# Scores and stored transposes in a mixer's tail, and a prompt's expert stage tied behind the other stream's linear attention

## The chip, the cores and the metric

The kernel runs on one core of a Trainium2 chip. The metric is the device time of one execution in microseconds (us). A core has five engines that each work through an instruction list of their own, in order: TensorE (PE, with its weight loads as PEld), VectorE (DVE), ScalarE (ACT), GpSimd (POOL) and SyncE (SP), which issues most DMAs.

## The reference

One inference step of a two-layer backbone on two streams: a prompt of 128 tokens, and a sample of 512 tokens in four blocks of 128 that also reads the prompt's cached keys, values and states. D is 1024. Each layer is a token mixer and an expert stage, each with a residual, conditioning factors and a LayerNorm.

```python
def token_mixer(...):
    q, k, v, gq, gk, gv, gout, glr, gmerge = jnp.split(h @ w_in, IN_SPLITS, axis=-1)
    ...
        attn = gqa_attend(q_r, jnp.concatenate([k_r, ctx_k], axis=1), jnp.concatenate([v, ctx_v], axis=1))
    o_f, s_f = gla_scan(gq, gk, gv, log_a[0], s0_f)
    o_b, s_b = gla_scan(jnp.flip(gq, 1), jnp.flip(gk, 1), jnp.flip(gv, 1), jnp.flip(log_a[1], 1), s0_b)
    ...
    y = (g_attn * (attn @ w_attn_o) + g_gla * (o @ w_gla_o)) @ w_out

def peer(h, wq, sub_keys, u, v):
    ...
        q = (xt @ wq).reshape(PEER_BLOCK, PEER_HEADS, 2, PEER_HALF)
        s = jnp.einsum('thpd,pnd->thpn', q, sub_keys).astype(jnp.float32)
        s1, i1 = lax.top_k(s[:, :, 0], PEER_TOPK)
        s2, i2 = lax.top_k(s[:, :, 1], PEER_TOPK)
        cand = (s1[..., :, None] + s2[..., None, :]).reshape(PEER_BLOCK, PEER_HEADS, PEER_TOPK * PEER_TOPK)
        sc, ci = lax.top_k(cand, PEER_TOPK)
        idx = jnp.take_along_axis(i1, ci // PEER_TOPK, axis=-1) * N_KEYS + jnp.take_along_axis(i2, ci % PEER_TOPK, axis=-1)
        g = jax.nn.softmax(sc, axis=-1)
        a = jax.nn.gelu(jnp.einsum('td,thkd->thk', xt, u[idx]).astype(jnp.float32))
        return jnp.einsum('thk,thkd->td', (g * a).astype(xt.dtype), v[idx])
```

Attention has 16 heads; linear attention (`gla_scan`) runs in both directions in chunks of 64. An expert stage has blocks of 128 tokens and 8 heads with two halves of 128 keys each; a head picks 16 of 16384 experts, which makes 128 dot products and 128 weighted sums per token.

## The kernel before, in words

**Stages of the sample.** Per layer the sample passes through its mixer (`mixer`, L253: linear attention, attention by groups of heads in 64 steps, the gated projections, the output projection with LayerNorm), then through its expert stage (`s_peer`, L1156). The mixer's tail projects the expert queries head by head (L779 to L791): 512 tokens at once into PSUM, a ScalarE copy to `q`, and a store of `q` to memory (`qTd`).

**Two ways through the expert stage.** Blocks 0 and 1 (`ROWS`) go by rows: GpSimd gathers, for each of the 128 chosen experts of a token, the row of `u` (`u_rows`, L911), VectorE makes a dot product of each (L917), then the same with the rows of `v` and weighted sums (`v_rows`, L947). Blocks 2 and 3 (`DENSE`) go densely (`dense`, L984): TensorE multiplies their 256 tokens with all 16384 rows of `u` (`hp`, in chunks), and with all of `v` (`vacc`). Between them stands a matrix of weights that VectorE spreads from the top-k (`spread`, L1051: `A` and `bw`, and matmuls `Gp`). The first `Gp` needs the complete top-k of both dense blocks. The dense blocks' input is loaded as rows from `h2d` and transposed on TensorE (L990 to L997).

**The top-k.** `front` (L804) takes a block's top-k in groups of heads: scores on TensorE (`sc`), two rounds of maxima on VectorE (`top16`, L796) from PSUM, the candidate sums, and one-hot steps that pick the indices (`oh`). For block 0 it runs in the query projection's loop and reads `q` where it lies (`near`); for the others SP loads `qT` from `qTd` (L820). The prompt has its own small top-k.

**The prompt.** Its single block goes by rows (`p_peer`, L1218): 128 dots and 128 weighted sums, beside the sample's next mixer. `merge` (L1233) interleaves the program's two tracks: each piece has an estimated length and a stretch in units of the sample's pieces (0 to 0.9 first mixer, 0.9 to 2 first expert stage, 2 to 2.9 second mixer, 2.9 to 4 second expert stage). The prompt's second expert stage has 2.03 to 2.75. The order that results is the order of each engine's list; `weave` does the same inside a stage, with the stretches `RF` and `FF` and the count `U0` of dots that lie in the projection loop. The prompt's gathers of a layer are also tied behind the sample's last gather of the layer before (`last_gather`, L898 and L905).

**Split weights.** The sample's weights come in two parts, `wh` (ScalarE copies) and `wl`, the rest that VectorE or GpSimd subtracts (L141).

## Time and profile before

| | |
|---|---|
| median of 3 runs | 5448.35 us (5431.43 to 5451.07) |
| profiled execution, its own time | 5425.23 us |
| span of the profile | 5423.5 us |
| TensorE busy | 4479.1 us (83%), mean granted clock 0.887 |
| VectorE busy | 3891.9 us (72%) |
| ScalarE, GpSimd busy | 1038.4 us (19%), 2199.4 us (41%) |
| moved by DMA | 1440.70 MB, 266 GB/s |

A busy share is a mean over stages with different limits. The stages of the second layer are: 2987 to 3036 us the end of layer 0, 3036 to 3516 linear attention, 3516 to 3771 attention, 3771 to 3980 gated projections, 3980 to 4063 output and LayerNorm, 4063 to 4177 query projection, top-k until the first `Gp` at 4490, dense blocks and row blocks to 5424. The prompt's second expert stage lies from 3017 to 3555. In layer 0 the attention's first 48 steps lie at 771 to 1070 and the gated projections at 1070 to 1345, there beside the prompt's first expert stage.

### The profile page before, as it was taken

What the parts mean: (1) busy time and instruction counts of PE and PEld (TensorE: products, weight loads), DVE (VectorE), ACT (ScalarE), POOL (GpSimd) and SP (SyncE); (2) the same over time, 40 slices, a digit from 0 to 9 for tenths busy, and PEclk for the clock granted to TensorE, in tenths of its full rate; (3) what the DMA queues carried; (4) which work ended last, traced back from release to release, by engine and by line L of the source; (5) the groups of instructions that cost most, each with busy time, mean ns of one, the idle gap of its engine ahead of it and who ended that gap; (6) DMA issues with size and microseconds to landing.
All of it is one profiled execution on the core that took longest, in us unless ns stands there. A gap on an engine that the chain in (4) does not pass through costs nothing.

```text
span 5423.5 us, 71661 instructions
## 1 busy us (share of the span) xinstructions
PE 4479.1 (83%) x26668; PEld 3365.0 (62%) x26668; DVE 3891.9 (72%) x8020; ACT 1038.4 (19%) x1876; POOL 2199.4 (41%) x1632
## 2 busy tenths in 40 slices
PE   7979878877766789799999477688977458998998
PEld 5658766755655657567674355588765347675643
DVE  4242578887699987948565999963258999979682
ACT  4231223412212101110000312255221010000000
POOL 0000026675255541544431576610115657255440
PEclk8989977888878889899999778789988779998999
DMA  5325669898489887899995788820447989699985
GB/s 185 118 70 179 235 225 327 305 338 297 171 318 348 317 317 258 310 357 334 382 344 206 244 309 297 290 91 29 131 146 271 329 305 362 225 399 325 409 327 197
DMA packets 472734, 1440.70 MB, mean 266 GB/s; under 512 B 55232, under 2 KB 123968, under 8 KB 472384
## 3 DMA queue, kind: packets, MB, share of 16 engines
q0 software_dynamic: 221184, 805.40, 40.5%
q1 hardware_dynamic: 251200, 630.71, 33.0%
q8 instruction: 209, 3.42, 0.2%
q14 instruction: 141, 1.16, 0.1%
HBM read 1391.29 MB, written 44.63 MB: 265 GB/s over the span
## 4 chain that ended last, share of the span: by engine, by line
PE 39%; DVE 26%; DMA 15%; issue 14%; POOL 4%; ACT 2%; SPq 0%; DVEq 0%; POOLq 0%; ACTq 0%
PE vacc L1096 7%; DVE gat L917 7%; PE gt L156 6%; PE proj L156 6%; DMA gat<-in_pv,idx 5%; PE hp L156 4%; DMA gat<-in_pu,idx 4%; POOL gat L900 4%; DVE acc L947 4%; PE po L156 3%; PE qp L156 2%; DMA v<-in_pv 2%; PE s L156 1%; PE gqk L156 1%; DVE A L1055 1%
## 5 line engine op out<-in xcount | busy, mean ns | idle before, releaser
L900 POOL DMA_INDIRECT gat<-in_pu,idx x768 | 982.3, 1279 | 884.9 <-DVE gat L917 378.7
L900 POOL DMA_INDIRECT gat<-in_pv,idx x768 | 989.4, 1288 | 765.1 <-DVE acc L947 472.9
L947 DVE SCALAR_TENSOR_TENSOR acc<-gat,dots,acc 128x1024 f32<-128x1024 f32 x762 | 1006.3, 1321 | 168.3 <-DMA gat<-in_pv,idx 156.1
L917 DVE SCALAR_TENSOR_TENSOR gat<-gat,h 128x1024 f32<-128x1024 f32 x768 | 948.4, 1247 | 110.8 <-DMA gat<-in_pu,idx 109.5
L156 PE MATMUL hp<-h2Td,uc 128*128 128x256 f32 x4096 | 942.5, 391 | 79.8 <-DVE wk L800 49.6
L1096 PE MATMUL vacc<-v,Q 128*128 128x512 f32 x2048 | 923.3, 604 | 17.2 <-DMA v<-in_pv 17.2
L156 PEld LDWEIGHTS hp<-h2Td,uc 128*128 128x128 f32 x4096 | 795.3, 196 | 200.2 <-DVE wk L800 52.3
L141 POOL TENSOR_TENSOR wl<-w,wh 128x1024 fp32r<-128x1024 f32 x92 | 227.5, 2473 | 1450.0 <-ACT wh L139 1279.5
L1096 PEld LDWEIGHTS vacc<-v,Q 128*128 128x128 f32 x2048 | 384.1, 193 | 459.4 <-issue 435.4
L139 ACT ACTIVATE wh<-w 128x1024 fp32r<-128x1024 f32 x184 | 194.4, 1058 | 631.9 <-PE proj L156 299.1
L1009 ACT ACTIVATE Q<-hp 128x512 f32<-128x512 f32 x128 | 76.4, 597 | 1069.6 <-PE hp L156 1069.3
L156 PE MATMUL proj<-wh,hTh 128*128 128x256 f32 x896 | 265.6, 296 | 5.6 <-DVE sgo L497 2.9
L156 PE MATMUL proj<-wl,hTh 128*128 128x256 f32 x896 | 264.7, 295 | 5.5 <-POOL wl L141 5.4
L156 PE MATMUL proj<-wh,hTl 128*128 128x256 f32 x896 | 262.8, 293 | 0.0
L1070 PEld LDWEIGHTS <-A 128*128 128x128 bf16 x6144 | 172.8, 97 | 125.7 <-DVE bw L1063 63.2
L156 PE MATMUL po<-V,pT 128*128 128x64 f32 x1600 | 237.9, 294 | 9.9 <-ACT pT L639 9.8
L156 PEld LDWEIGHTS po<-V,pT 128*128 128x128 f32 x1600 | 229.2, 217 | 24.9 <-ACT pT L639 16.7
L1070 PE MATMUL Gp<-bw,A 128*128 128x32 bf16 x6144 | 175.8, 177 | 73.3 <-DVE bw L1063 64.1
L141 DVE TENSOR_TENSOR wl<-w,wh 128x1024 fp32r<-128x1024 f32 x92 | 121.0, 1315 | 158.7 <-ACT wh L139 148.4
L629 DVE TENSOR_REDUCE nm<-s 128x1 f32<-128x768 f32 (+1 forms) x160 | 131.0, 820 | 139.9 <-PE s L156 138.5
L156 PEld LDWEIGHTS proj<-wh,hTh 128*128 128x128 f32 x896 | 176.9, 197 | 20.4 <-issue 16.2
L156 PEld LDWEIGHTS proj<-wl,hTh 128*128 128x128 f32 x896 | 176.9, 197 | 20.4 <-issue 13.8
(297 smaller groups left out, 7355.5 us busy)
## 6 DMA issues: line engine op xcount, KB each, us to landing
uc<-in_put SPq DMA_DIRECT2D x256, 512.0 KB, 7.0
v<-in_pv SPq DMA_DIRECT2D x256, 512.0 KB, 6.7
w<-in_win SPq DMA_DIRECT2D x208, 512.0 KB, 5.1
w<-in_adaw SPq DMA_DIRECT2D x96, 512.0 KB, 5.7
w<-in_wq SPq DMA_DIRECT2D x64, 512.0 KB, 5.8
w<-in_wgo SPq DMA_DIRECT2D x32, 512.0 KB, 5.5
w<-in_wao SPq DMA_DIRECT2D x32, 512.0 KB, 5.2
w<-in_wout SPq DMA_DIRECT2D x32, 512.0 KB, 5.5
```

The source lines that it names most:

```text
L139: nc.scalar.activation(wh, r, AF.Copy)
L141: (nc.vector, nc.gpsimd)[i].tensor_sub(wl, r, f32(wh))
L156: nc.tensor.matmul(out, lt, rt, start=(i == 0), stop=(i == n - 1))
L629: nc.vector.tensor_reduce(nm, s[:, 0:KEYS], axis=AX.X, op=OP.max, negate=True)
L900: i = nc.gpsimd.indirect_dma_start(out=t, out_offset=None, in_=src, in_offset=bass.IndirectOffsetOnAxis(ap=self.res[b][0][:, k:k + 1], axi ...
L917: nc.vector.scalar_tensor_tensor(u, u, 1.0, h2, op0=OP.mult, op1=OP.mult, accum_out=dots[:, k:k + 1])
L947: nc.vector.scalar_tensor_tensor(acc, v, w_, acc, op0=OP.mult, op1=OP.add)
L1009: nc.scalar.activation(q[:, i:i + 2, :].rearrange("p i t -> p (i t)"), t, AF.Gelu_apprx_tanh)
L1055: nc.vector.tensor_tensor(a.rearrange("p t (i w) -> p t i w", w=2), pairs[:, None].to_broadcast([128, TG, NK // 2, 2]), i1[:, sl, None, :] ...
L1070: nc.tensor.matmul(t[:, j * CI:(j + 1) * CI], a[:, j, :], bw[:, j, q, :], start=(q == 0), stop=(q == 2))
L1096: nc.tensor.matmul(accs[i][:, s * 512:(s + 1) * 512], w[:, j, i * 128:(i + 1) * 128], v[:, s * 512:(s + 1) * 512], start=(key == 0), stop= ...
```

## The change

**1. Scores in the mixer's tail.** After a head's two query projections the loop also computes the scores of all four blocks, and ScalarE copies them to `sc` in SBUF. Block 0's stay there; those of blocks 1 to 3 are stored, by ScalarE's DMA queue, to `scd`. `q` of the sample is no longer stored. `front` of these blocks loads 128 KB of scores (`scs`), also on ScalarE's queue, and `top16` reads them from SBUF, so that no matmul stands in it.

```diff
-                    nc.sync.dma_start(qTd[2 * h + k], q)
+                if tr:
+                    yield 11
+                    for b0 in range(0, nb, 2):
+                        s = psm("sc", 1)
+                        for i in range(2):
+                            for k in range(2):
+                                nc.tensor.matmul(s[:, (2 * i + k) * NK:(2 * i + k + 1) * NK],
+                                                 qs[k][:, (b0 + i) * 128:(b0 + i + 1) * 128],
+                                                 lp[l]["sk"][:, k, :], start=True, stop=True)
+                        sc = hp.tile([128, 2, 2 * NK], F32, tag="sc", bufs=4, name="sc")
+                        nc.scalar.activation(sc.rearrange("p b n -> p (b n)"), s, AF.Copy)
+                        for i in range(2):
+                            if b0 + i == ROWS[0]:
+                                lp[l]["s", h] = sc[:, i, :]
+                            else:
+                                nc.scalar.dma_start(scd[b0 + i, :, h * 2 * NK:(h + 1) * 2 * NK], sc[:, i, :])
...
+                elif tr:
+                    s = own.tile([128, 2 * NK], F32, tag="scs", bufs=2, name="scs")
+                    nc.scalar.dma_start(s, tops[tr, l][b, :, hh * 2 * NK:(hh + 1) * 2 * NK])
```

**2. Order of the dense blocks' top-k.** Their fronts work in groups of two heads and are woven into the projection loop (three of four groups each), the rest follows at once; `U0` falls, so fewer dots lie in the loop.

```diff
+NEXT = (2, 2, 2, 2)
-FF = (0.05, 0.1, 0.3, 0.46)
+FF = (0.01, 0.02, 0.3, 0.46)
-U0 = 56
+U0 = 24
+            fd = [p.front(d, NEXT) for d in DENSE]
-                for n in LEAD:
-                    yield from take(m, n)
+                for i, n in enumerate(LEAD):
+                    yield from take(m, 2 * n)
                     yield from take(f0, 3 * n + 1)
+                    if i >= 2:
+                        for f in fd:
+                            yield from take(f, 3 * NEXT[i - 2] + 1)
```

**3. The dense blocks' input stored transposed.** ScalarE copies the transposes that LayerNorm's end makes anyway (`hc`) and SP stores them to `h2t_dram`; `dense` loads them in one DMA.

```diff
+                        if kept:
+                            hc = spare("hc")
+                            nc.scalar.activation(hc[:, 0:jg * 128], t, AF.Copy)
+                            i = DENSE.index(b)
+                            nc.sync.dma_start(h2t_dram[l][:, j0:j0 + jg, i * 128:(i + 1) * 128],
+                                              hc[:, 0:jg * 128].rearrange("p (j t) -> p j t", j=jg))
...
-            for i, b in enumerate(blocks):
-                x = dp.tile([128, D], F32, tag="uv", bufs=UB, name="x")
-                nc.sync.dma_start(x, h2_dram[self.tr, self.l][b * 128:(b + 1) * 128, :])
-                t = psb("h2td")
-                for j in range(ND):
-                    nc.tensor.transpose(t[:, j * 128:(j + 1) * 128], x[:, j * 128:(j + 1) * 128], ident)
-                evac(h2T[:, :, i * 128:(i + 1) * 128], t.rearrange("p (j t) -> p j t", j=ND))
-                yield 4
+            nc.sync.dma_start(h2T, h2t_dram[self.l])
```

**4. The prompt's second expert stage.** Its stretch moves, and its gathers are tied behind the latest GpSimd instruction of the sample, a gather or a subtraction `wl`, in place of the latest gather.

```diff
-           (wait(("s_done", 0)), 1000.0, 1.95, 2.0), (p_peer(1), 386.0, 2.03, 2.75)])
+           (wait(("s_done", 0)), 1000.0, 1.95, 2.0), (p_peer(1), 386.0, 2.36, 2.86)])
-            after = last_gather.get(self.l - 1) if self.tr == 0 else None
+            after = last_pool.get("ins") if self.tr == 0 and self.l else None
```

GpSimd, from the last gather of the sample's first layer on (gathers of `in_pu` rows are for the dots, of `in_pv` rows for the sums). Before:

```order
L900 DMA gat<-in_pv,idx 128x1024 x128
L141 TENSOR_TENSOR wl<-w,wh 128x1024
L900 DMA gat<-in_pu,idx 128x1024 x17
L141 TENSOR_TENSOR wl<-w,wh 128x1024
L900 DMA gat<-in_pu,idx 128x1024 x11
L141 TENSOR_TENSOR wl<-w,wh 128x1024
L900 DMA gat<-in_pu,idx 128x1024 x5
```

And after:

```order
L937 DMA gat<-in_pv,idx 128x1024 x128
L143 TENSOR_TENSOR wl<-w,wh 128x1024 x15
L937 DMA gat<-in_pu,idx 128x1024 x9
L143 TENSOR_TENSOR wl<-w,wh 128x1024
L937 DMA gat<-in_pu,idx 128x1024 x52
L143 TENSOR_TENSOR wl<-w,wh 128x1024
L937 DMA gat<-in_pu,idx 128x1024 x47
L143 TENSOR_TENSOR wl<-w,wh 128x1024
```

The first gather for the prompt stood behind one weight part and now stands behind fifteen, those of the linear attention.

VectorE in the scan of the second linear attention (`S` is the recurrent state, L917 the prompt's dots). Before:

```order
L482 SCALAR_TENSOR_TENSOR S<-S,ee,kv 128x256 x2
L917 SCALAR_TENSOR_TENSOR gat,dots<-gat,h_22584 128x1024 x2
L482 SCALAR_TENSOR_TENSOR S<-S,ee,kv 128x256
L141 TENSOR_TENSOR wl<-w,wh 128x1024
L917 SCALAR_TENSOR_TENSOR gat,dots<-gat,h_22584 128x1024
L482 SCALAR_TENSOR_TENSOR S<-S,ee,kv 128x256 x2
L917 SCALAR_TENSOR_TENSOR gat,dots<-gat,h_22584 128x1024 x2
L482 SCALAR_TENSOR_TENSOR S<-S,ee,kv 128x256
```

And after:

```order
L426 TENSOR_TENSOR a<-eb,gq 128x512
L143 TENSOR_TENSOR wl<-w,wh 128x1024
L424 TENSOR_TENSOR m<-m,gk 128x512
L449 COPY_PREDICATED amat_22622<-masks,A 128x512
L449 COPY_PREDICATED amat_22624<-masks,A 128x512
L487 SCALAR_TENSOR_TENSOR S<-S,ee,kv 128x256 x12
L143 TENSOR_TENSOR wl<-w,wh 128x1024
L487 SCALAR_TENSOR_TENSOR S<-S,ee,kv 128x256 x2
```

No dot stands between the updates of the state any more.

TensorE from the last query projection to the first matmuls of the dense blocks (`hp`), layer 1. Before:

```order
L156 MATMUL qp<-h2Th,wl 128x512
L825 MATMUL sc<-sk,q 128x128 x2
L825 MATMUL sc<-sk,qT 128x128 x2
L995 MATMUL h2td<-ident,x 128x128 x16
L825 MATMUL sc<-sk,qT 128x128 x6
L156 MATMUL hp<-h2Td,uc 128x256 x43
L825 MATMUL sc<-sk,qT 128x128 x2
L156 MATMUL hp<-h2Td,uc 128x256 x5
```

And after:

```order
L160 MATMUL qp<-h2Tl,wh 128x512
L160 MATMUL qp<-h2Th,wl 128x512
L814 MATMUL sc<-sk,q 128x128 x8
L160 MATMUL hp<-h2Td,uc 128x256 x256
L1069 MATMUL kT<-ident,kf 128x128 x2
L1070 MATMUL kT<-ident,g 128x128
```

The transposes and the score matmuls of the dense blocks are gone from the front of `hp`; `kT` transposes the finished top-k of a dense block.

## Rows read from the trace of the kernel before

**Rows 1.** the chain of waits, share of the span by engine

```profile
PE 39%; DVE 26%; DMA 15%; issue 14%; POOL 4%; ACT 2%; SPq 0%; DVEq 0%; POOLq 0%; ACTq 0%
```

**Rows 2.** windows: length, busy time of each engine, TensorE's granted clock, DMA share, GB/s

```profile
2987.00:3036.00 49.00, 8.99 (x38) 7.32 (x38) 47.28 (x167) 16.55 (x27) 12.30 (x9) 0.57 0.56 194
3036.00:3516.00 480.00, 345.66 (x1758) 260.35 (x1758) 438.88 (x657) 114.96 (x175) 341.97 (x249) 0.80 0.86 299
3516.00:3771.00 255.00, 225.30 (x1708) 213.57 (x1708) 139.95 (x253) 138.62 (x292) 27.53 (x18) 0.89 0.20 63
3771.00:3980.00 209.00, 192.70 (x867) 156.71 (x866) 53.66 (x67) 60.65 (x82) 38.27 (x16) 0.97 0.38 121
4080.00:4490.00 410.00, 231.07 (x970) 188.01 (x969) 396.65 (x1194) 47.42 (x68) 252.46 (x192) 0.77 0.87 311
4490.00:4880.00 390.00, 381.30 (x2853) 288.83 (x2850) 345.39 (x656) 25.41 (x38) 194.71 (x144) 0.98 0.88 329
```

**Rows 3.** groups on VectorE, linear attention: busy us, mean ns, idle before, releasers

```profile
L917 DVE SCALAR_TENSOR_TENSOR gat<-gat,h 128x1024 f32<-128x1024 f32 x124 | 162.0, 1324 | 15.2 <-DMA gat<-in_pu,idx 14.8
L947 DVE SCALAR_TENSOR_TENSOR acc<-gat,dots,acc 128x1024 f32<-128x1024 f32 x107 | 145.9, 1363 | 7.3 <-DMA gat<-in_pv,idx 5.1 <-ACT acc L945 1.2
L917 DVE DVE_READ_ACCUMULATOR gat<-gat,h 128x1 f32 x124 | 9.7, 78 | 0.0
```

**Rows 4.** waits of TensorE in the linear attention: us, times, longest

```profile
PE ksT L426 <- DVE m L419: 52.6, 8, 20.8
PE oTp L505 <- DVE sgo L500: 19.2, 2, 10.2
```

**Rows 5.** groups on VectorE, attention of layer 1

```profile
L947 DVE SCALAR_TENSOR_TENSOR acc<-gat,dots,acc 128x1024 f32<-128x1024 f32 x20 | 25.5, 1277 | 0.2
```

**Rows 6.** groups on VectorE, top-k stretch of layer 1, 4080 to 4490

```profile
L917 DVE SCALAR_TENSOR_TENSOR gat<-gat,h 128x1024 f32<-128x1024 f32 x128 | 158.5, 1243 | 8.0 <-DMA gat<-in_pu,idx 7.9
L947 DVE SCALAR_TENSOR_TENSOR acc<-gat,dots,acc 128x1024 f32<-128x1024 f32 x50 | 63.6, 1273 | 0.8 <-DMA gat<-in_pv,idx 0.6
L843 DVE TENSOR_TENSOR cand<-tv 128x16 f32<-128x16 f32 (+11 forms) x63 | 11.2, 219 | 0.0
```

**Rows 7.** groups on VectorE, first 48 steps of layer 0's attention, 771 to 1070

```profile
L917 DVE SCALAR_TENSOR_TENSOR gat<-gat,h 128x1024 f32<-128x1024 f32 x127 | 154.7, 1235 | 4.5 <-DMA gat<-in_pu,idx 4.4
L947 DVE SCALAR_TENSOR_TENSOR acc<-gat,dots,acc 128x1024 f32<-128x1024 f32 x10 | 12.8, 1278 | 2.1 <-ACT acc L945 1.9
```

**Rows 8.** windows of layer 0's attention and gated stage

```profile
771.00:1070.00 299.00, 254.42 (x1713) 203.96 (x1713) 259.71 (x472) 115.06 (x242) 187.86 (x139) 0.79 0.89 320
1070.00:1345.00 275.00, 206.64 (x811) 161.20 (x809) 224.22 (x201) 60.07 (x77) 183.75 (x129) 0.84 0.88 318
```

**Rows 9.** groups on VectorE, gated stage of layer 0

```profile
L947 DVE SCALAR_TENSOR_TENSOR acc<-gat,dots,acc 128x1024 f32<-128x1024 f32 x117 | 171.2, 1463 | 27.1 <-DMA gat<-in_pv,idx 24.9
```

**Rows 10.** groups on TensorE, gated stage of layer 0

```profile
L156 PE MATMUL gt<-gxh,wh 128*128 128x512 f32 x128 | 55.6, 454 | 42.3 <-ACT gxh L271 42.3
```

**Rows 11.** groups on TensorE, gated stage of layer 1, 3771 to 3980

```profile
L156 PE MATMUL gt<-gxh,wh 128*128 128x512 f32 x128 | 50.1, 408 | 12.2 <-ACT gxh L271 12.2
```

**Rows 12.** groups on TensorE, top-k stretch of layer 1, 4080 to 4490

```profile
L156 PE MATMUL hp<-h2Td,uc 128*128 128x256 f32 x512 | 126.3, 411 | 41.2 <-DVE wk L800 24.3 <-issue 15.3 <-ACT Q L1009 1.6
L825 PE MATMUL sc<-sk,qT 128*128 128x128 f32 x64 | 16.0, 393 | 85.6 <-DVE wk L800 43.8 <-DMA qT<-qTd 39.7 <-ACT Q L1009 2.1
L825 PE MATMUL sc<-sk,q 128*128 128x128 f32 x31 | 6.4, 286 | 2.5 <-ACT q L785 2.4
L1070 PE MATMUL Gp<-bw,A 128*128 128x32 bf16 x17 | 0.6, 188 | 12.6 <-DVE bw L1063 12.6
```

**Rows 13.** groups on ScalarE, whole span

```profile
L785 ACT ACTIVATE q<-qp 128x512 f32<-128x512 f32 x32 | 18.7, 590 | 70.4 <-PE qp L156 70.4
```

**Rows 14.** DMA issues, whole span: KB each, median us to landing

```profile
qT<-qTd SPq DMA_DIRECT2D x64, 128.0 KB, 4.2
```

**Rows 15.** groups of the page, whole span

```profile
L1070 PE MATMUL Gp<-bw,A 128*128 128x32 bf16 x6144 | 175.8, 177 | 73.3 <-DVE bw L1063 64.1
```

More of the change, by code (lines that the diff above doesn't have):

```diff
@@ L119 @@
     lp = {}
+    last_pool = {}
     class Weights:
@@ L140, in __call__ @@
                 wl = self.pool.tile([128, 4, CW], F32R, tag="wl", bufs=3, name="wl")
-                (nc.vector, nc.gpsimd)[i].tensor_sub(wl, r, f32(wh))
+                ins = (nc.vector, nc.gpsimd)[i].tensor_sub(wl, r, f32(wh))
+                if i:
+                    last_pool["ins"] = ins.ins
                 h.append(wh)
@@ L314, in mixer @@
         x1_dram[tr, l], h2_dram[tr, l] = x1d, h2d
+        if tr:
+            h2t_dram[l] = dram.tile([128, ND, len(DENSE) * 128], F32, name=f"h2t{l}")
         ys_ = ExitStack()
@@ L696, in mixer @@
             yield from ada(l, (GATE1, SCALE2, SHIFT2, GATE2), W)
-        qTd = dram.tile([2 * PH, 128, T], F32, name=f"qTd{tr}{l}")
-        tops[tr, l] = qTd
+        if tr:
+            scd = dram.tile([nb, 128, PH * 2 * NK], F32, name=f"scd{l}")
+            tops[tr, l] = scd
+        else:
+            qTd = dram.tile([2 * PH, 128, T], F32, name=f"qTd{tr}{l}")
+            tops[tr, l] = qTd
         with mkp("out") as op:
@@ L757, in mixer @@
                     nc.vector.tensor_add(h2, h2, sh)
-                    nc.sync.dma_start(h2d[b * 128:(b + 1) * 128, :], h2)
+                    kept = tr == 1 and b in DENSE
+                    if not kept:
+                        nc.sync.dma_start(h2d[b * 128:(b + 1) * 128, :], h2)
                     for j0 in range(0, ND, jg):
@@ L780, in mixer @@
                 t = ptile("qp")
+                qs = []
                 for k in range(2):
                     projT(t[:, k * off:k * off + T], w, k, h2T)
-                    q = hp.tile([128, T], F32, tag="q", bufs=2 + 2 * tr, name="q")
+                    q = hp.tile([128, T], F32, tag="q", bufs=2 + tr, name="q")
                     if tr:
@@ L816, in front @@
                 if near:
-                    qs = [lp[l]["q", tr, 2 * hh + k][:, b * 128:(b + 1) * 128] for k in range(2)]
+                    s = lp[l]["s", hh]
+                elif tr:
+                    s = own.tile([128, 2 * NK], F32, tag="scs", bufs=2, name="scs")
+                    nc.scalar.dma_start(s, tops[tr, l][b, :, hh * 2 * NK:(hh + 1) * 2 * NK])
                 else:
@@ L821, in front @@
                                       .rearrange("k p t -> p k t"))
-                    qs = [qT[:, k, :] for k in range(2)]
-                s = psm("sc", tr)
-                for k in range(2):
-                    nc.tensor.matmul(s[:, k * NK:(k + 1) * NK], qs[k], lp[l]["sk"][:, k, :], start=True, stop=True)
+                    s = psm("sc", tr)
+                    for k in range(2):
+                        nc.tensor.matmul(s[:, k * NK:(k + 1) * NK], qT[:, k, :], lp[l]["sk"][:, k, :],
+                                         start=True, stop=True)
                 for k in range(2):
@@ L903, in gather @@
             if self.tr == 1:
[L904 removed]
+                last_pool["ins"] = i.ins
             return t
@@ L1162, in s_peer @@
             r0, r1 = ROWS
-            d0, d1 = DENSE
             f0, u0 = p.front(r0, LEAD, True), p.u_rows(r0)
+            fd = [p.front(d, NEXT) for d in DENSE]
             def lead():
-                for n in LEAD:
-                    yield from take(m, n)
+                for i, n in enumerate(LEAD):
+                    yield from take(m, 2 * n)
                     yield from take(f0, 3 * n + 1)
+                    if i >= 2:
+                        for f in fd:
+                            yield from take(f, 3 * NEXT[i - 2] + 1)
                 for _ in m:
                     pass
-            yield from weave([(lead(), 160.0, 0.0, 1.0)], [(take(u0, U0), 1.5 * U0, UP, 1.0)])
+            yield from weave([(lead(), 260.0, 0.0, 1.0)], [(take(u0, U0), 1.5 * U0, UP, 1.0)])
             for _ in f0:
@@ L1183, in s_peer @@
                               (p.u_rows(r1), 192.0, r[2], r[3]), (p.v_rows(r1), 197.0, r[3], r[4])],
-                             [(p.front(d0), 50.0, 0.0, f[0]), (p.front(d1), 50.0, f[0], f[1]),
-                              (p.front(r1), 50.0, f[2], f[3])])
+                             [(fd[0], 12.5, 0.0, f[0]), (fd[1], 12.5, f[0], f[1]), (p.front(r1), 50.0, f[2], f[3])])
         fs = parts["fin"] = ExitStack()
```

12 lines of the change are left out of this document (7 added, 5 removed).

## The prediction

> **What bounds the kernel now.** I read the chain of waits by engine first [rows 1]: TensorE 39%, VectorE 26%, DMA 15%, so no single engine is the bound throughout, and a change must be priced stage by stage. I then cut the part that the change touches, the sample's second layer, into stretches [rows 2]. The reader is to see who is full in each. 2987 to 3036 (residual and LayerNorm of layer 0): VectorE 47.28 of 49 us. 3036 to 3516 (linear attention): VectorE 438.88 of 480, TensorE only 345.66 at a granted clock of 0.80. 3516 to 3771 (attention): TensorE 225.30 of 255, VectorE 139.95. 3771 to 3980 (the gated projections): TensorE 192.70 of 209 at 0.97, VectorE 53.66. 4080 to 4490 (query projection and top-k ahead of the dense blocks): VectorE 396.65 of 410. From 4490 the dense blocks: TensorE 381.30 of 390. So VectorE bounds the linear attention and the top-k, TensorE the rest.
>
> What fills VectorE in the linear attention is not the sample's own work. The groups of that stretch [rows 3] show 124 dot products of the prompt's expert stage (162.0 us, and 9.7 us of accumulator reads) and 107 weighted sums (145.9 us). TensorE meanwhile waits [rows 4]: 52.6 us on `m` and 19.2 us on `sgo`, both VectorE tiles that queue behind prompt work.
>
> **The change part by part.** Baseline is the profiled execution, 5425.23 us (span 5423.5); the median of the runs is 23.1 us higher, so I add 23 at the end.
>
> *The prompt's second expert stage goes behind the second linear attention.* By the instruction order, of the 128 dots 16 come between the scan and attention, 112 in attention's first 48 head steps of 64; 26 sums lie in those steps, none in the last 16, 97 in the gated stage, the last 5 ahead of LayerNorm.
>
> Settle: 4 of the 128 dots ran before 3036, on a full VectorE. At about 1.3 us each that is -5 us (bounds -10 and 0).
>
> Linear attention: VectorE keeps 438.88 - 162.0 - 9.7 - 145.9 = 121 us, plus 16 dots (21 us), far under the stage's length, so TensorE is late next. Its 345.66 us at 0.80 become 345.66 x 0.80 / 0.97 = 285 us at the clock that the gated stage had when no prompt work stood beside it. Of its 134 us of idle I keep a third, 45 us, for the recurrence and for ScalarE. 480 becomes 330: -150 us. Lower bound: no idle left, 285 us, -195. Upper: clock unchanged and only the two VectorE waits gone, 480 - 52.6 - 19.2 = 408 us, -72.
>
> Attention: VectorE's own work is 139.95 less 20 sums (25.5 us [rows 5]) = 114.5 us. Added are 112 dots at 1.238 us and 0.078 us of accumulator read [rows 6, 3], 147.4 us, and 26 sums at 1.273 us, 33.1 us; the prices of dot and sum are from the top-k stretch [rows 6], where VectorE was full. In the first 48 steps that is 0.75 x 114.5 + 180.5 = 266 us; at the 97% that VectorE reaches when it bounds (396.65 of 410) 275 us. The last 16 are TensorE's: 225.30 x 0.89 / 0.97 / 4 = 52 us. Sum 327, +72 us. Layer 0 bounds it from above: there attention ran beside 127 dots and 10 sums [rows 7] and its first 48 steps took 299 us, TensorE at 0.79 [rows 8]: 299 + 52 = 351, +96. From below, if VectorE had no gap: 114.5 + 180.5 = 295, +40.
>
> Gated stage: layer 0 again has the case, 1070 to 1345 [rows 8]: 275 us against 209, with 117 sums at 1463 ns [rows 9], TensorE's wait for `gxh` 42.3 us in place of 12.2 [rows 10, 11], clock 0.84 in place of 0.97. That is 66 us for 117 sums; for 97, +55 us. Bounds: 66 above; below 0, because 53.66 + 97 x 1.273 = 177 us would still fit into 209.
>
> In the gated stage a sum takes 1463 ns, beside GpSimd's subtractions `wl`, and 1273 ns in the top-k stretch [rows 6, 9]. The Trainium skill, "SBUF — State Buffer", section "Who interferes with whom", says that a VectorE instruction with two SBUF inputs and a GpSimd instruction that reads SBUF exclude one another on a shared port, and that TensorE and ScalarE wait for nobody there. The longer sums of the gated stage agree. By that rule alone the stage would lose only the lock time and the sum would be that of rival B; by layer 0's whole stage it loses 55 us.
>
> *Scores in the tail.* Per layer the projection loop gains 48 score matmuls for three blocks (64 for four, 16 for one before) at 6.4 / 31 = 0.21 us [rows 12], 10 us of TensorE, and 16 ScalarE copies of about 0.59 us, as `q` has [rows 13], 9 us. Both lie beside a full VectorE, so most is hidden; 24 stores and 24 loads of 128 KB also pass through ScalarE's instruction stream. The loads wait for a buffer that VectorE must free, and behind a waiting load stand the copies that release TensorE. A load of that size took 4.2 us to land [rows 14]. I take +5 us per layer, +10 (bounds -5 and +25). The 32 stores of `q` leave SP, off any full engine: nothing.
>
> *Top-k of the dense blocks.* The 85.6 us that TensorE idled ahead of `sc<-sk,qT` and the 41.2 ahead of `hp` [rows 12] vanish as such: the 256 `hp` now follow without a break. But they open nothing: the first `Gp` needs all the top-k, and VectorE was full in that stretch. So I count VectorE's work ahead of it in both orders. Layer 0: 10 sums fewer (-13 us), about 120 more small top-k operations at 0.22 us [rows 6] (+26 us) since groups of two heads replace groups of four, 32 more maxima at the same price (+7): +20. Layer 1: 30 sums fewer (-38), the small operations +26, seven one-hot steps at no more than a dot's 1.3 us (+9): -3. Later TensorE waited 64.1 us for `bw` over both layers [rows 15], of which 12.6 was the first `Gp` of layer 1 [rows 12]; taking as much for layer 0, about 40 remain, met where block 1's top-k stood in front of the second spread. That top-k is now earlier; I take half, -20. Together -3 us (bounds -40: all 40 and nothing added; +35: VectorE's 20 in layer 0, and 15 more in layer 1, if its sums merely move).
>
> *Stored transposed input.* 16 transposes (3.4 us at the 0.21 us of a small matmul) and two evacuations leave the dense blocks' start, two ScalarE copies come in per layer, the store goes out where the row store did, and one load takes the place of two. TensorE idles over 100 us there [rows 12], so 0; without that cover the 3.4 us per layer would be gained.
>
> Sum: -5 - 150 + 72 + 55 + 10 - 3 = -21 us. 5425 - 21 = 5404 for a profiled execution, 5427 against the median.
>
> **Rivals.**
>
> *A, the attention and gated stages become VectorE's.* VectorE executes in order, so the row maximum that releases the next score tile, and the subtraction behind `gxh`, stand behind 1.3 us operations. For: layer 0 shows just this pairing, with TensorE at 0.79 and 0.84. Against: layer 0 also loaded the conditioning weights there (320 GB/s in its row against 63), which layer 1 doesn't. Attention +96, gated +66, and the linear attention loses only the wait for `m`: 285 + 134 - 53 = 366, -114. Sum -5 - 114 + 96 + 66 + 10 - 3 = +50: 5498. It decides once the linear attention takes over 340 us beside stages as in layer 0.
>
> *B, the sums fit into the gated stage's gaps.* Then it grows only by what the sums take longer there than elsewhere, 97 x (1463 - 1273) ns = 18 us, the rest as forecast: -21 - 37 = -58: 5390. The rule of the Trainium skill named above would have it so. For: VectorE is idle 155 of 209 us, and the sums' own gathers don't compete with other loads. Against: layer 0's 42.3 us on `gxh`.
>
> *C, ScalarE's queue blocks.* The 24 loads per layer hold the copies behind them. If each of the waits for `qT` (within the 85.6 us) comes back as a wait of VectorE on its scores, some 40 us per layer: +80 on the forecast, 5507. For: two buffers and one in-order queue. Against: most loads stand behind the last projection copies.
>
> *D, the tie moves the work without effect*, gain and price equal: 5448. TensorE would keep its low clock in the linear attention.
>
> **How the numbers follow.** The shortest difference that the measurement separates from no change is about 0.5%, 27 us: faster means under 5421, slower over 5476. Forecast 0.48, its own band 5395 to 5460, of it 0.22 under 5421; A 0.17; B 0.20; C 0.10 (0.07 at over 49 us, which ends slower, 0.03 below that); D 0.05. Faster: 0.22 + 0.20 = 0.42. Same: 0.26 + 0.05 + 0.03 = 0.34. Slower: 0.17 + 0.07 = 0.24. The terms' bounds as half widths (5, 61, 28, 33, 15, 37) add in squares to 85; I take 5360 to 5500, which leaves out C's full price, and the case where linear attention meets its lower bound in B.
>
> **What the profile would show.** The linear attention near 330 us with no prompt dot in its scan and a granted clock over 0.9; attention near 327 and the gated stage near 264 us; first `Gp` of layer 1 as far behind the first projection as before; no `sc<-sk,qT`. The forecast is wrong if the linear attention stays over 380 us, if the gated stage doesn't grow, or if VectorE waits on `scs`.

## The result and the profile after

The changed kernel is slower: 5479.48 us, median of 5 runs (5476.02 to 5484.05), against 5448.35 us; ratio 1.0064, 95% interval 1.0048 to 1.0079. The forecast was 5427 us, within 5360 to 5500: the sign was wrong, by a margin that the range allowed for. The profiled execution took 5484.05 us, 58.8 more than that of before. Of these some 25 belong to the profiled execution of before, which lay 6 us below the fastest of its other runs: profiled again (e1 below) the unchanged kernel had a span of 5439.5 us, and the changed one (e5) 5473.5.

Windows of the changed kernel, over the stages of [rows 2]: settle, linear attention, attention, gated stage, output and LayerNorm, top-k until the first `Gp`, dense blocks. Columns as there.

```profile
3017.00:3060.00 43.00, 10.49 (x48) 8.09 (x46) 42.97 (x173) 16.77 (x27) 2.59 (x1) 0.56 0.43 144
3060.00:3421.00 361.00, 310.01 (x1759) 238.48 (x1760) 178.76 (x337) 113.13 (x177) 61.57 (x37) 0.92 0.26 86
3421.00:3746.00 325.00, 241.03 (x1704) 221.25 (x1704) 264.03 (x462) 136.30 (x288) 168.69 (x136) 0.83 0.67 234
3746.00:4017.00 271.00, 207.12 (x843) 163.60 (x842) 182.63 (x160) 59.89 (x81) 165.02 (x116) 0.85 0.78 285
4017.00:4113.00 96.00, 56.45 (x416) 53.63 (x415) 69.45 (x99) 21.40 (x21) 10.44 (x5) 0.78 0.51 180
4130.00:4549.00 419.00, 218.43 (x971) 182.67 (x970) 398.82 (x1448) 59.54 (x90) 207.80 (x162) 0.77 0.76 270
4549.00:4940.00 391.00, 380.31 (x2864) 286.04 (x2865) 328.31 (x457) 22.57 (x35) 215.16 (x155) 0.98 0.92 340
```

The work moved as the order said. The linear attention lost 120 us (480 to 361), VectorE is no longer full there (178.76 us), and TensorE's clock rose from 0.80 to 0.92, not to 0.97. The attention took 325 us in place of 255, the gated stage 271 in place of 209. Within the attention the first 48 steps and the last 16 were:

```profile
3419.00:3706.00 287.00, 201.26 (x1368) 182.97 (x1368) 247.25 (x438) 108.78 (x228) 169.91 (x138) 0.80 0.76 264
3706.00:3748.00 42.00, 42.00 (x358) 40.51 (x356) 19.74 (x29) 30.64 (x67) 0.00 (x0) 1.00 0.04 11
```

The waits of TensorE in the linear attention show what is late next:

```profile
PE ksT L431 <- DVE m L424: 14.7, 6, 4.4
PE kTp L565 <- ACT kd L560: 12.4, 2, 12.1
```

The wait for `m` fell from 52.6 us [rows 4] to 14.7. The prompt's dots and sums on VectorE, first in the attention, then in the gated stage; before, the attention had 20 sums [rows 5] and the gated stage none:

```profile
L954 DVE SCALAR_TENSOR_TENSOR gat<-gat,h 128x1024 f32<-128x1024 f32 x111 | 133.9, 1219 | 10.7 <-DMA gat<-in_pu,idx 9.8 <-issue 0.3
L984 DVE SCALAR_TENSOR_TENSOR acc<-gat,dots,acc 128x1024 f32<-128x1024 f32 x26 | 33.4, 1283 | 2.6 <-DMA gat<-in_pv,idx 2.3
```

```profile
L984 DVE SCALAR_TENSOR_TENSOR acc<-gat,dots,acc 128x1024 f32<-128x1024 f32 x97 | 134.7, 1389 | 34.5 <-DMA gat<-in_pv,idx 32.7
```

In the gated stage TensorE waits for `gxh` as in layer 0 [rows 10, 11], and behind it ScalarE waits for the loads of `xraw`: first the group on TensorE, then two waits of ScalarE.

```profile
L160 PE MATMUL gt<-gxh,wh 128*128 128x512 f32 x128 | 53.6, 438 | 38.0 <-ACT gxh L274 38.0
```

```profile
ACT gxh L274 <- DMA xraw<-aod: 36.9, 8, 13.4
ACT gxh L274 <- DMA xraw<-ood: 32.2, 7, 12.6
```

In the kernel before, the same two waits came to 15.5 and 15.6 us.

TensorE and VectorE in the top-k stretch, against [rows 12, 6], and the page's row on `Gp` against [rows 15]:

```profile
L160 PE MATMUL hp<-h2Td,uc 128*128 128x256 f32 x512 | 123.6, 407 | 149.7 <-ACT Q L1040 83.8 <-DMA uc<-in_put 65.9
```

```profile
L984 DVE SCALAR_TENSOR_TENSOR acc<-gat,dots,acc 128x1024 f32<-128x1024 f32 x20 | 25.5, 1276 | 0.1
L835 DVE MAX8 tv<-wk 128x8 f32<-128x128 f32 x64 | 17.9, 284 | 0.0
L880 DVE TENSOR_TENSOR cand<-tv 128x16 f32<-128x16 f32 (+10 forms) x103 | 14.6, 184 | 0.0
```

```profile
L1101 PE MATMUL Gp<-bw,A 128*128 128x32 bf16 x6144 | 178.0, 177 | 76.1 <-DVE bw L1094 64.5
```

The wait for `qT` is gone, but `hp` now waits for `Q`, a ScalarE tile: that is TensorE's old slack under another name, since VectorE was busy 398.82 of 419 us. It had 20 sums there in place of 50, but 64 rounds of maxima in place of 48 and 103 candidate sums in place of 63. The wait for `bw` did not fall (64.1 to 64.5 us).

By stage, in us; "second pair" are the profiles of e1 and e5:

| stage | forecast | first pair | second pair |
|---|---|---|---|
| layer 0 until its query projection | 0 | +15.2 | -0.8 |
| layer 0, query projection to end of settle | +10 | +8.6 | +0.5 |
| linear attention | -150 | -120.4 | -121.8 |
| attention, gated stage, output, LayerNorm | +127 | +146.7 | +144.4 |
| layer 1, query projection to end | -8 | +8.7 | +11.7 |
| sum | -21 | +58.8 | +34.0 |

The second pair's sum is near the +31 of the medians, so I go by it; the 15 us ahead of layer 0's query projection were chance. Its two profiles come from two chips, but e1's profiled execution (5441.32 us) lies at the median of the kernel before on e5's chip (5442.11 us).

### The profile page after: what moved, and what is told of

Its sections match the earlier page's. It is cut to its first block, busy times and chain, and to the rows that moved or that the text cites. A ratio compares the mean times of both kernels' runs of the same rounds, so it can differ in the third digit from the quotient of the medians.

```text
span 5482.3 us, 71820 instructions
## 1 busy us (share of the span) xinstructions
PE 4440.9 (81%) x26636; PEld 3342.6 (61%) x26636; DVE 3905.8 (71%) x8202; ACT 1064.6 (19%) x1923; POOL 2150.0 (39%) x1632
## 4 chain that ended last, share of the span: by engine, by line
PE 32%; DVE 29%; issue 16%; DMA 14%; POOL 6%; ACT 3%; SPq 0%; another core or an unknown queue 0%; POOLq 0%; DVEq 0%; ACTq 0%
DVE gat L954 8%; DMA gat<-in_pv,idx 7%; PE vacc L1127 6%; PE proj L160 6%; PE gt L160 5%; POOL gat L937 5%; PE hp L160 3%; DMA gat<-in_pu,idx 3%; DVE acc L984 3%; PE po L160 2%; PE gqk L160 2%; DVE A L1086 2%; DVE Q L1106 1%; PE s L160 1%; DVE bw L1094 1%
## 5 line engine op out<-in xcount | busy, mean ns | idle before, releaser
L937 POOL DMA_INDIRECT gat<-in_pv,idx x768 | 956.3, 1245 | 892.9 <-DVE acc L984 588.7
L937 POOL DMA_INDIRECT gat<-in_pu,idx x768 | 963.6, 1255 | 823.0 <-DVE gat L954 416.2
L1101 PE MATMUL Gp<-bw,A 128*128 128x32 bf16 x6144 | 178.0, 177 | 76.1 <-DVE bw L1094 64.5
L487 DVE SCALAR_TENSOR_TENSOR S<-S,ee,kv 128x256 f32<-128x256 f32 x128 | 61.4, 479 | 177.9 <-PE kv L475 177.7
```

The costliest lines, as they stand in the source:

```text
L487: nc.vector.scalar_tensor_tensor(S2, S[d], ee_[d][:, cc:cc + 1], kv[d][:, 0:DV], op0=OP.mult, op1=OP.add)
L937: i = nc.gpsimd.indirect_dma_start(out=t, out_offset=None, in_=src, in_offset=bass.IndirectOffsetOnAxis(ap=self.res[b][0][:, k:k + 1], axi ...
L1101: nc.tensor.matmul(t[:, j * CI:(j + 1) * CI], a[:, j, :], bw[:, j, q, :], start=(q == 0), stop=(q == 2))
```

## The experiments

T1 is the reading of the stage table: the tie's loss of 147 us behind the linear attention outweighs its gain. R2 is its rival: the tie gains, and the scores and their order lose. Ratios are against runs of the kernel before on the same chip, in brackets their 95% intervals.

**e1, the kernel before once more.**

> The unchanged kernel once more, for a second profile. Theory T1 (the changed kernel's first layer is really slower ahead of its dense blocks) expects the stage map of the first profile: first query projection of layer 0 at about 1428 us, of layer 1 at 4063. Rival R1 (some 25 of the 59 us between the two profiles belong to the profiled run of before, which lay 23 us under its median) expects a span near 5446 and these points 10 to 25 us later. Ratio 1.000 within 0.003 by both.

Measured: 0.9996 (0.9981 to 1.0011), span 5439.5 us, first query projections at 1435.0 and 4076.8. Nearer to R1, at less than it expected: these points came 6.6 and 13.5 us later than in the first profile, and nothing under some 15 us per stage can be read from a single pair.

**e2, the tie alone** (part 4 on the kernel before).

```diff
-            after = last_gather.get(self.l - 1) if self.tr == 0 else None
+            after = last_pool.get("ins") if self.tr == 0 and self.l else None
...
-           (wait(("s_done", 0)), 1000.0, 1.95, 2.0), (p_peer(1), 386.0, 2.03, 2.75)])
+           (wait(("s_done", 0)), 1000.0, 1.95, 2.0), (p_peer(1), 386.0, 2.36, 2.86)])
```

> The kernel before with part 4 alone (prompt's second expert stage at 2.36 to 2.86 and tied behind the latest GpSimd instruction). Theory T1, from the stages of the changed kernel's profile: linear attention -120 us, attention and gated stage +136, output and LayerNorm +11, settle -7, so +20 us, ratio 1.004, and the linear attention at about 360 us. Rival R2 (the tie gains, scores and order lose): -20 us, 0.996. Forecast on record: -28 us.

Measured: 1.0039 (1.0025 to 1.0053), +21 us. T1 held, R2 fell: the part of the change on which the forecast's gain rested loses by itself. Its windows, linear attention, attention and gated stage, are those of the changed kernel:

```profile
3040.00:3400.00 360.00, 310.59 (x1762) 238.57 (x1762) 176.03 (x334) 113.09 (x177) 62.27 (x38) 0.92 0.26 86
3400.00:3729.00 329.00, 241.84 (x1714) 222.69 (x1712) 264.60 (x463) 137.57 (x291) 174.37 (x136) 0.82 0.67 231
3729.00:3995.00 266.00, 203.01 (x839) 159.60 (x839) 185.96 (x161) 58.98 (x80) 165.99 (x117) 0.87 0.80 291
```

**e3, the changed kernel without the tie** (e2's edit undone).

> The changed kernel without part 4. T1: what remains of the changed kernel's +31 us once the tie's +20 is out: about +11 us, ratio 1.002, linear attention near 480 us again. R2: +50 us, 1.009. A third possibility, that parts 1 to 3 gain and the tie loses it all: below 0.998.

Measured: 1.0067 (1.0053 to 1.0081), more than T1's 1.002 and less than R2's 1.009. So parts 1 to 3 lose too, and the losses of e2 and e3 don't add up to that of the whole (1.0064 here, 1.0064 in e5). T1 was half the story; the next runs take the other half apart.

**e4, the stored transposed input alone** (part 3 on the kernel before).

> The kernel before with part 3 alone (transposed input stored in the mixer's tail, no transposes in the dense blocks). Forecast on record: 0 us. Rival R3 (the two copies by ScalarE lie on the path from LayerNorm to the query projection, which starts 15 and 19 us later in the changed kernel): up to +10 us per layer, ratio 1.002 to 1.004, with the first query projection later by that much from the gated stage's end.

Measured: 1.0000 (0.9986 to 1.0013). As forecast, nothing in the total, where R3 fell. But the place that R3 named does show: from the first output projection to the first query projection it took 89.8 us in layer 0 and 91.3 in layer 1, against 85.7 and 87.3 in e1. What gives these 4 us per layer back, or whether they vanish in the interval, was not tested.

**e5, the changed kernel once more.**

> The changed kernel once more, beside the next three on one chip. All theories: ratio 1.006 within 0.002, linear attention about 360 us, attention to query projection about 690 us, the first A of the dense blocks 404 to 421 us behind the first query projection.

Measured: 1.0064 (1.0045 to 1.0083); linear attention 361.1 us, from there to the query projection 690.5, first A 421.4 and 405.6 us behind it.

**e6, stored scores and input without the new order of the fronts.** T4: part 2 is what makes parts 1 to 3 slow; R4: the stored scores are. The edit, on e3:

```diff
-FF = (0.01, 0.02, 0.3, 0.46)
+FF = (0.05, 0.1, 0.3, 0.46)
...
-U0 = 24
+U0 = 56
...
-                    if i >= 2:
-                        for f in fd:
-                            yield from take(f, 3 * NEXT[i - 2] + 1)
...
-                             [(fd[0], 12.5, 0.0, f[0]), (fd[1], 12.5, f[0], f[1]), (p.front(r1), 50.0, f[2], f[3])])
+                             [(p.front(d0), 50.0, 0.0, f[0]), (p.front(d1), 50.0, f[0], f[1]), (p.front(r1), 50.0, f[2], f[3])])
```

> The changed kernel without parts 2 and 4: scores and transposed input from the tail, the dense blocks' top-k in groups of four heads and not in the projection loop, the prompt as before. By its instruction order VectorE has ahead of the first A 103 dots and no sum where the kernel before has 144 and 16 (layer 0) or 159 and 31 (layer 1). Theory T4 (part 2 is what makes parts 1 to 3 slow, by the extra groups and the block 1 heads that it puts ahead of the first A) expects no loss against before, ratio 0.990 to 1.000, and the first A 50 to 90 us earlier behind the first query projection. Rival R4 (the stored scores themselves, by ScalarE's queue, cost it) expects 1.004 to 1.010 and VectorE waiting on scs.

Measured: 0.9992 (0.9979 to 1.0005). T4's main point held, and R4 fell: without part 2, storing scores and input costs nothing that can be measured. But the first A, 64 us earlier in layer 0 and 99 in layer 1, brought nothing: the first `Gp` came 453 and 426 us behind the query projection (e1: 425 and 428). In the 128 and 134 us between A and `Gp` stand 25 dots, 23 to 29 sums and one-hot steps for another 8 to 10 heads. What counts is what stands ahead of the first `Gp`, not of the first A.

**e7, the new order of the fronts alone** (part 2 on the kernel before, with `qT` loads).

> The kernel before with part 2 alone: fronts of the dense blocks in groups of two heads in the projection loop, U0 24, with qT loads and score matmuls as before. Its order has 182 dots, 54 sums and 13 groups ahead of the first A (before: 144 to 159, 16 to 31, 9). T4: the first A 50 to 100 us later per layer, part of it given back in the dense blocks, ratio 1.005 to 1.015. R4: ratio 1.000 within 0.003.

Measured: 1.0231 (1.0211 to 1.0251), worse than T4 expected: first `Gp` 524 and 475 us behind the query projection, 99 and 47 later than in e1. R4 fell. Parts 1 and 2 interact: with scores at hand the new order costs 0.7%, with `qT` loads 2.3%.

**e8, the tie with short operations.** A test of rival A of the prediction: is it VectorE's occupation that lengthens the attention and the gated stage? The edit, on e2, with the like of it for the weighted sums:

```diff
+                c = 64 if self.tr == 0 and self.l == 1 else D
-                nc.vector.scalar_tensor_tensor(u, u, 1.0, h2, op0=OP.mult, op1=OP.mult, accum_out=dots[:, k:k + 1])
+                nc.vector.scalar_tensor_tensor(u[:, 0:c], u[:, 0:c], 1.0, h2[:, 0:c], op0=OP.mult, op1=OP.mult,
+                                               accum_out=dots[:, k:k + 1])
```

> The kernel before with part 4 alone, and the prompt's dots and weighted sums of layer 1 over 64 of 1024 columns (it leaves out the rest of these sums; all gathers stay). If VectorE's occupation is what makes the attention and gated stages longer (forecast, rival A of the prediction), their growth of about 136 us goes nearly all, they take 255 and 209 us again, and the ratio is 0.975 to 0.980. Rival R5 (gathers, memory traffic and the lower TensorE clock make it): they stay over 300 and 250 us, ratio over 0.995.

Measured: 0.990 (0.9875 to 0.9926). Neither: attention and gated stage fell only to 302 and 256 us, though VectorE was idle over half of both. (The profiled execution was the slowest of the four, 13 us over their median.)

```profile
3398.00:3700.00 302.00, 244.47 (x1708) 225.75 (x1709) 131.96 (x477) 137.33 (x291) 140.83 (x142) 0.85 0.74 260
3700.00:3956.00 256.00, 203.69 (x856) 162.30 (x854) 84.86 (x162) 61.07 (x82) 138.02 (x117) 0.87 0.82 306
```

In the gated stage the waits for `xraw` were 59 us (69 in e2, 31 in e1): the gathers keep them long. In the attention VectorE, with these short operations, stood 23 us waiting for gathered rows:

```profile
L920 DVE SCALAR_TENSOR_TENSOR gat<-gat,h 128x64 f32<-128x64 f32 x118 | 23.3, 218 | 26.2 <-DMA gat<-in_pu,idx 18.8 <-issue 7.5
L952 DVE SCALAR_TENSOR_TENSOR acc<-gat,dots,acc 128x64 f32<-128x64 f32 x26 | 7.2, 278 | 4.4 <-DMA gat<-in_pv,idx 4.1
```

**e9, the tie with few gathers.** On e2, with the like of it for the rows of v:

```diff
+                if k % 8 == 0 or self.tr == 1 or self.l == 0:
-                u = self.gather(pu, b, k)
+                    u = self.gather(pu, b, k)
```

> The kernel before with part 4 alone, and the prompt's stage of layer 1 gathers only every eighth row of u and v (it computes the other dots and sums from the row at hand, so the other rows are left out); all 256 VectorE operations stay. In the run with short operations the growth of attention and gated stage went down by only 42 of 139 us. Theory T5 (the gathers do the rest: their traffic delays the loads of xraw that gxh waits for in the gated stage, and VectorE waits in order for late rows) expects xraw waits back near 31 us from 68, the gated stage and output back to 300 us from 360, ratio 0.985 to 0.995. Rival R6 (VectorE's occupation): gated stage and output over 340, ratio over 0.998.

Measured: 1.005 (1.003 to 1.0071). The ratio settles nothing, since the edit moved the dots: 72 of them ran on VectorE ahead of the first attention step (17 in e2), and TensorE waited for them to pass. The longest wait of TensorE there:

```profile
PE kTp L562 <- ACT kd L557: 87.5, 1, 87.5
```

The stages themselves can still be read. The first 48 steps of the attention, in e1, e8 and e9:

```profile
3530.00:3742.00 212.00, 183.13 (x1358) 172.86 (x1359) 120.05 (x222) 108.87 (x227) 27.11 (x18) 0.87 0.23 73
3397.00:3655.00 258.00, 202.38 (x1367) 185.96 (x1366) 110.57 (x436) 108.41 (x227) 130.49 (x131) 0.82 0.78 276
3460.00:3729.00 269.00, 184.71 (x1364) 173.44 (x1363) 189.64 (x331) 108.57 (x227) 19.67 (x14) 0.79 0.11 39
```

With all gathers and short operations (e8) TensorE was busy 19 us longer than in e1 and idle 27 us longer. With few gathers and full operations (e9, 56 dots and 31 sums left in the attention) its busy time stayed and the idle grew by 55 us. So each lengthens the attention in its own way.

The gated stage took 242 us with `xraw` waits of 43, in between e1 and e2; with the output stage it came to 325 us, between T5's 300 and R6's 340. TensorE's wait for `gxh` is back at that of e1 (12.5 us; e2 39.7), and its wait for VectorE's `sg` is up from 1.9 us:

```profile
PE gt L159 <- DVE sg L679: 18.4, 7, 5.4
PE gt L159 <- ACT gxh L273: 12.4, 5, 8.9
```

**e16, both.**

> Part 4 alone on the kernel before, with the prompt's layer 1 operations over 64 of 1024 columns and only every eighth row gathered (the rest of both is left out). If gathers and VectorE's occupation make the longer stages between them, attention takes about 255 us and gated stage to query projection about 295 us, as in the kernel before without prompt work, with the linear attention still near 360: ratio 0.972 to 0.978. If both stages stay 30 us or more longer, something else (order on VectorE, the TensorE clock by itself) is at work.

Measured: 0.979 (0.9776 to 0.9805). Linear attention, attention, gated stage:

```profile
3031.00:3383.00 352.00, 310.73 (x1759) 239.25 (x1758) 163.79 (x427) 112.64 (x176) 47.12 (x24) 0.93 0.22 71
3383.00:3642.00 259.00, 225.20 (x1709) 213.87 (x1710) 124.50 (x375) 137.95 (x291) 18.40 (x14) 0.88 0.12 43
3642.00:3866.00 224.00, 195.23 (x855) 156.67 (x853) 87.98 (x181) 61.80 (x83) 50.72 (x28) 0.95 0.46 152
```

The attention is back at 259 us, the gated stage at 224, 17 above e1. So VectorE's occupation and the gathers together make the longer stages, and either alone keeps a large part of it: of the attention's 75 us some 48 stay with gathers alone, of the gated stage's 59 some 49. Why TensorE is busy longer beside the gathers, and how much of its idle comes from VectorE waiting in order for late rows, was not taken apart further. The output stage to the query projection took 85 us, as before.

**e10, the tie with the old stretch** (2.03 to 2.75), which by the order spreads the prompt's work over all three stages. The new stretch without the tie would leave the order of instructions on every engine as it was; the tie is what moves it.

> The kernel before with the new tie, but the old stretch 2.03 to 2.75. By its order some 130 dots lie in the linear attention, about 91 sums in the attention, the rest in the gated stage: the prompt's work spread over three stages. If each dot or sum costs the same wherever it stands (about 0.5 us each: 122 us for some 240 in the linear attention, 139 us for 256 behind it), the ratio is 1.000 to 1.004. If the cost comes from a full VectorE (linear attention 439 of 480 us before, attention's first 48 steps after), the spread avoids it: -30 to -60 us, 0.989 to 0.995.

Measured: 0.9991 (0.9978 to 1.0004): linear attention 420.7 us, to the query projection 599.1, both between those of e1 and e2. No gain that can be measured: the spread did not relieve a full VectorE as I had hoped. The 214 operations that e2 moves cost 124 us in the linear attention, 0.58 us each, and 139 behind it, 0.65 us. The 106 that e10 moves cost 62 us there, 0.59 us each, and 53 behind it, 0.50 us. By these profiles the other 108 would cost 0.80 us each behind it, a hint that the price rises as the stages fill; with stages uncertain by some 15 us it is no more than that.

**e11, scores without the new order, and e10's tie.**

> The changed kernel without part 2 (dense top-k in groups of four, not in the projection loop) and with the old stretch 2.03 to 2.75 under the new tie. Expected as the sum of the two: scores without part 2 measured -0.1%, so the ratio of the run before it less 0.001; 0.989 to 0.994 if the spread helps, about 1.000 if each operation costs the same everywhere.

Measured: 0.9959 (0.9941 to 0.9976), between the two expectations and clear of both 1.000 and 0.994. The sum of e6 and e10 would be 0.998; where the rest comes from was not tested.

**e12, groups of four.** On e3:

```diff
-NEXT = (2, 2, 2, 2)
+NEXT = (4, 4)
...
-                    if i >= 2:
+                    if i == 2:
                         for f in fd:
-                            yield from take(f, 3 * NEXT[i - 2] + 1)
+                            yield from take(f, 3 * NEXT[0] + 1)
...
-                             [(fd[0], 12.5, 0.0, f[0]), (fd[1], 12.5, f[0], f[1]), (p.front(r1), 50.0, f[2], f[3])])
+                             [(fd[0], 25.0, 0.0, f[0]), (fd[1], 25.0, f[0], f[1]), (p.front(r1), 50.0, f[2], f[3])])
```

> The changed kernel without part 4 and with the dense blocks' top-k in groups of four heads, one group each still in the projection loop. Its order has 10 groups, 24 to 26 one-hot steps and 112 to 118 dots ahead of the first A, no sum; with groups of two (1.0067 measured) 14 groups, 25 one-hot steps, 139 to 143 dots and 11 to 15 sums. T4 in its strict form (what stands on VectorE ahead of the first Gp counts): first Gp some 40 to 55 us earlier than with groups of two, ratio 0.996 to 1.001. Rival: the position in the projection loop itself costs, ratio over 1.004.

Measured: 0.9875 (0.9855 to 0.9895), 67 us faster than the kernel before, more than T4 expected. Top-k stretch of layer 1 until the first `Gp`, as a window and by groups on VectorE, first of e3:

```profile
4089.00:4526.00 437.00, 235.50 (x1030) 196.12 (x1030) 400.29 (x1449) 62.58 (x93) 208.22 (x162) 0.77 0.74 260
```

```profile
L952 DVE SCALAR_TENSOR_TENSOR gat<-gat,h 128x1024 f32<-128x1024 f32 x128 | 161.6, 1272 | 15.0 <-DMA gat<-in_pu,idx 14.8
L982 DVE SCALAR_TENSOR_TENSOR acc<-gat,dots,acc 128x1024 f32<-128x1024 f32 x20 | 25.5, 1276 | 0.1
L878 DVE TENSOR_TENSOR cand<-tv 128x16 f32<-128x16 f32 (+10 forms) x103 | 14.6, 183 | 0.0
```

And of e12:

```profile
4036.00:4421.00 385.00, 231.91 (x1030) 193.46 (x1030) 355.23 (x1288) 55.47 (x84) 173.51 (x139) 0.81 0.74 261
```

```profile
L952 DVE SCALAR_TENSOR_TENSOR gat<-gat,h 128x1024 f32<-128x1024 f32 x126 | 154.3, 1230 | 7.5 <-DMA gat<-in_pu,idx 7.4
L878 DVE TENSOR_TENSOR cand<-tv 128x32 f32<-128x32 f32 (+11 forms) x70 | 11.2, 199 | 0.0
```

VectorE has 45 us less to do ahead of the first `Gp`: no sum of the row blocks stands there any more, and a third of the small steps is gone. The first `Gp` comes 52 us earlier, and the rest of the layer follows as fast (949.8 us from the first A to the last `vacc`, e1: 953.2). But the execution ends 36 us behind the last `vacc` in place of 18: of the chain's last 227 us 61.8% are gathers of `in_pv` rows for the row blocks' sums, against 17.1% of the last 240 in e1. So the row blocks become the end of layer 1, and of the 52 us some 27 arrive there. Layer 0 gains the same way, 385 in place of 423 us to the first A.

**e13, groups of two, two of four in the loop.** On e3:

```diff
-                    if i >= 2:
+                    if 2 <= i < 4:
...
-                             [(fd[0], 12.5, 0.0, f[0]), (fd[1], 12.5, f[0], f[1]), (p.front(r1), 50.0, f[2], f[3])])
+                             [(fd[0], 25.0, 0.0, f[0]), (fd[1], 25.0, f[0], f[1]), (p.front(r1), 50.0, f[2], f[3])])
```

> The changed kernel without part 4, groups of two heads, with two of four groups of each dense block in the projection loop instead of three. Its order ahead of the first A is nearly that of the run without the tie: 98 candidate sums, 14 groups, 137 to 141 dots, 9 to 13 weighted sums. Theory T6 (the group size is what costs): 1.005 to 1.008. Rival (the share in the loop costs): 0.987 to 0.995, as with groups of four.

Measured: 1.0029 (1.0017 to 1.0041). Between the two, and nearer to T6: of the 1.9% between e3 and e12 the group size makes 1.5, the share in the loop 0.4.

**e14 and e15, groups of four with the tie** as the change has it, and with e10's.

> The changed kernel whole, but with groups of four heads. T6: the changed kernel's 1.0064 falls by the 1.9% that separated groups of two from groups of four without the tie, to 0.988. If the tie costs on top what it costs alone (0.4%): 0.991 to 0.993; if nothing, as groups of two suggested (1.0064 with tie, 1.0067 without): 0.987 to 0.988.

Measured: 0.9911 (0.9897 to 0.9925). The tie costs 0.4% here too, as alone.

> Groups of four with the new tie, but the old stretch 2.03 to 2.75. Alone the early tie measured 0.9991, on top of the scores -0.3%. Expected 0.984 to 0.988, the lowest of all; if the spread of the prompt's work gains nothing, 0.987 to 0.988.

Measured: 0.987 (0.9851 to 0.989), 5360.48 us. With e12 the fastest version run that leaves nothing out; the two can't be told apart.

## Why the prediction was wrong

The miss is 55 us, from -21 forecast to +34 by the second pair: 28 in the linear attention, 17 in the three stages behind it and 20 in layer 1's expert stage, less 10 in layer 0's.

*Linear attention, -150: the failed step.* Its mechanism was right (the prompt's work out of the scan, VectorE free, TensorE's wait for `m` gone) and its size wrong: measured -122, 28 us of the miss. The idle was 361 - 310 = 51 us against 45 assumed. The error was the step that took TensorE's busy time from 345.66 us to 285, where 310 came. It scaled the busy time by the mean granted clocks of two stretches, 0.80 and 0.97, and a mean over a stretch takes in its idle time. Weighted by the durations of the matmuls, the traces give 0.865 in this stretch before and 0.961 after: 345.66 x 0.865 / 0.961 = 311 us. e9 shows it from the other side: with an idle wait of 87.5 us inside the stretch its mean clock was 0.85, and TensorE was busy 311.06 us all the same.

*Attention, +72.* The number held, partly by luck. From the first row maxima to the first gated projection the attention grew by 72 us in the first pair and by 75 in the second. But the forecast had its first 48 steps bound by VectorE at 97% and 275 us long; they took 287, with VectorE busy 247.25 us, 86%. The last 16, put at 52 us, took 42. Two errors, +12 and -10 us, cancelled. That VectorE's occupation alone makes the growth was wrong too: e8 kept most of it with short operations.

*Gated stage, +55, and what follows.* The gated stage grew by 65 us in the first pair and 63 in the second; layer 0's pairing was the right model. Output and LayerNorm, for which the sum had no term, grew by another 9 and 7. The last four sums and the prompt's own LayerNorm stand there on VectorE (with the tie alone, e2, the stage grew by 3), and ScalarE's copies `hc` stand there too (e4, without the tie: 4). With the attention's 3 this is 17 us of the miss, 144 in place of 127.

*Top-k, -3 in both layers with half of the wait for `bw` back.* Layer 0 gave back by its end what it lost (+0.5, forecast +10). In layer 1 the first `Gp` came 9 to 10 us later. My count of VectorE's work had the sums right (-38) but left the added maxima out there, and in layer 0 counted one instruction for a round of five: between e1 and e5 the five of a round together grew by 25 us per layer. In all VectorE was busy 4 us longer ahead of layer 1's first `Gp` (396.39 to 400.68), where -3 was counted, and 26 us longer in layer 0 (396.74 to 423.16), where +20 was. The wait for `bw` stayed at 64 us, so the -20 didn't come. Half of that and the later `Gp` are most of the miss of 20 in layer 1.

*Scores in the tail, `hc` and `h2T`.* The +10 for the scores did not show: parts 1 and 3 without part 2 (e6) measured 0.9992. The zero for the stored input held in the total (e4), not in the output stage, as said. Rival C fell: in the changed kernel's trace VectorE never waits for `scs`. The forecast that `hp` would follow without a break failed, since ScalarE did block in order, though behind VectorE: TensorE's wait of 77.8 us for one `Q` came while ScalarE waited 41.9 and 26.9 us for two `g` of the top-k, which stood ahead of that `Q`. It fell into a stretch in which VectorE was full, so I count it as TensorE's slack; no run tests that.

*Rivals.* A was the nearest, at 5498 against 5479 measured: the linear attention over 340 us (361) beside stages as in layer 0, the point from which it was to decide. Its cause was half right, since the gathers do about as much as VectorE. D was near for the tie by itself: gain and price differ by 15 us (124 and 139, e2). B fell: the sums did not fit into the gaps. In the gated stage a sum took 1389 ns against 1283 in the attention, 10 us for 97, of a stage that grew by 65. The rest shows in e2 against e1: there TensorE waited 27 us longer for `gxh`, behind the loads of `xraw`, 13 for VectorE's `gxl`, 4 for `sg`, and was busy 12 us longer. The Trainium skill ("SBUF — State Buffer", section "Who interferes with whom") says that only the shared port pair causes contention, by an exclusive lock. By it alone the 10 us would have been all. The trace doesn't speak against the rule: the other waits are of another kind, for late loads and for an engine that works through its list in order.

The chance of 0.24 on slower held what came. The forecast's weakness was its shape: a sum of -21 as the difference of 150 and 127, the first with bounds of some 61 us to either side, the two terms of the second with 28 and 33.

## What to carry to other kernels

Moving a filler stage from one place to another is worth the difference of two prices, and here an operation cost 0.58 us in one and 0.65 in the other; measure both before the sign is trusted. To price a change of TensorE's clock, take the clock of its busy time, not the mean of a stretch in which it idles: here 0.865 against 0.80. Ahead of an operation that needs a complete top-k, count every instruction that stands before it on the full engine, the filler work between included, and beware of small groups: two heads to a group cost 1.5% against four (larger ones were not run). A moved step takes its DMA traffic along, and loads that were quick in the quiet stage become the new wait.

## What the runs showed of the hardware

The gathers alone, with VectorE nearly free of the prompt's work, lengthened the attention from 254 to 302 us (e8) with TensorE's granted clock at 0.85 in place of 0.89, though it moves little by DMA itself (62 GB/s in e1). With 285 to 306 GB/s moved in the gated stage the loads of `xraw` kept ScalarE waiting 59 to 69 us, with 138 to 152 GB/s 39 to 43 us (e9, e16), with 121 GB/s 31 us. And executions of one kernel on one chip spread over 42 us (5410 to 5452 us), more than the change itself.
